# Attention probabilities turned by VectorE in 32x32 blocks and placed by a trip through DRAM, in place of TensorE transposes and copies

## The chip, the cores and the metric

The kernel runs on one core of one Trainium2 chip. The metric is the device time of the whole program in microseconds (us). Before the change it is 2019.93 us, the median of three runs from 2014.48 to 2020.14 us.

The names used below: TensorE (PE) does the matrix products, VectorE (DVE), ScalarE (ACT) and GpSimd (POOL) do the work on elements, and SyncE (SP) issues nearly all transfers, in the order of its own queue. SBUF is the memory on the chip that the engines work in, PSUM holds what TensorE writes, DRAM is the memory off the core. The granted clock is the share of TensorE's full clock that the throttle let it have.

## The reference, cut to what matters

The program is one layer of a hybrid encoder for 1024 tokens of width 1024: a layer norm, one projection to 11776 columns, dilated attention in three groups, a gated recurrence (HGRN2), a merge, a second norm and a SwiGLU feed-forward block. The change touches the attention alone. In the reference, for each group (a window and a dilation) and each of eight heads:

```python
s = jnp.einsum('nbqhd,nbkhd->nbhqk', qb, kb) * (dh ** -0.5)
s = jnp.where(valid, s + bias, NEG_INF)
mx = jnp.max(s, axis=-1, keepdims=True)
p = jnp.exp(s - mx)
l = jnp.sum(p, axis=-1, keepdims=True)
o = jnp.einsum('nbhqk,nbkhd->nbqhd', p, vb) / jnp.transpose(l, (0, 1, 3, 2, 4))
...
w = jax.nn.softmax(jnp.stack(lses), axis=0)
o = jnp.sum(w[..., None] * jnp.stack(outs), axis=0)
```

Everything is in float32.

## The kernel before

**The large products.** Every big product is split into three float32r products (hi by hi, hi by lo, lo by hi), in `mm3` (lines 275 to 279): three TensorE instructions of 128x128 weights by 512 columns for each 128 rows of depth. The projection is computed with a seven-product scheme on 2x2 blocks: `stream` (from line 677) walks over 23 groups of four column tiles, and for each group and each of two halves `g` it does seven products of 12 instructions. I call 12 such instructions a **step**; a group is 14 steps. For each half the four weight blocks a11, a12, a21 and a22 (256 KB each) are loaded on SP's queue by `block` (L256 is the load), when the block that held the place has been used. For the product numbered 6 VectorE first adds and subtracts blocks (L717, L718), so that it needs a11, a21 and a22; ScalarE then makes the hi part (L219) and GpSimd the lo part (L229). The results leave PSUM through VectorE or ScalarE into one of three `evh` buffers and are stored to DRAM on SP's queue (L578, L592, L605, L620).

**The side units.** While the projection streams, `phase1` runs side units between the steps: two recurrence units and two attention units for each of four pairs of heads. A unit is a generator; `yield 2` in it means that its next part is emitted two steps later. The order that the engines get is made from this by a list scheduler with priorities, so instructions of a unit can be put later than they were emitted.

**Attention of a pair j of heads.** `att_far` handles the two dilated groups, and `att_near` the undilated one. In each, TensorE computes scores with the queries on the partitions (L885, L902; near L1032 to L1035), VectorE adds the bias and takes the row maximum (`ttr`, L826), ScalarE takes the exponential in place with the row sums (L922; near L1051). The far probabilities lie in six tiles named `pf` (three of 1024 columns, two of which 896 columns and one of which 256 columns are used), the near ones in four tiles `p` of 1024 columns. The product with V needs the keys on the partitions, so every 128x128 block is turned first: `turn1` and `turn2` (L932, L940) for the far side and a loop at L1091 for the near side do it with 40 and 32 TensorE transposes a pair, 288 in all. They go to PSUM banks of the pool `sd` (four banks for all side units), and `copied` brings them back into the tile they came from, half of them by VectorE (L843), half by ScalarE (L841). Then come the products with V (far L963, L968, L972; near L1107) and, on the far side, a small product that reorders the row statistics (L987).

**What is queued where.** SP's queue holds the weight loads, the stores of `evh`, and the fetches for the side units, in one order; each of its transfers may wait for a semaphore, and those behind it wait as well.

Of the kernel before, what the change touches and what calls it, by code (L numbers as in the profile page):

```python
# [10 lines left out]
F32 = mybir.dt.float32  # L11
# [9 lines left out]
T = 1024  # L21
# [58 lines left out]
class Block:  # L80
    evac_ahead = 1000

    def __init__(self, ctx, tc, x, ln_in_g, ln_in_b, w_in, hgrn_lb, hgrn_norm_g, w_att_up, w_hgrn_up,
# [8 lines left out]
        nc = self.nc  # L92
# [24 lines left out]
                     for j in range(4)]  # L117
        for h in range(8):
            self.hg_d[h]["v"] = dram.tile([T, 128], F32, name=f"hg{h}v")
        for j in range(4):  # L120
            self.at_d[j].update({("v", g): dram.tile([T, 128], F32, name=f"at{j}v{g}") for g in range(3)})
        self.w_d = [dram.tile([32, 128], F32, name=f"wd{j}") for j in range(4)]
# [681 lines left out]
    def fetch_rows(self, n, name, src, g=0):  # L804
# [49 lines left out]
    def att_far(self, j, qk):  # L854
# [68 lines left out]
                                             accum_out=l[:, hd, c:c + 1])  # L923
        nc.vector.tensor_add(L12, L12, LB)
        yield 2
        yield 2

        def turn1(r):
            for hd in range(2):
                ps, p = self.ps_sd(), P1(r, hd)  # L930
                for n in range(3):
                    nc.tensor.transpose(ps[:, 128 * n:128 * n + 128], p[:, 128 * n:128 * n + 128], ident)  # L932
                self.copied(hd, p, ps[:, 0:384])

        def turn2(r0):
            for hd in range(2):
                ps = self.ps_sd().rearrange("p (r e c) -> p r e c", r=2, e=2)
                for r in range(2):
                    for e in range(2):
                        nc.tensor.transpose(ps[:, r, e], P2(r0 + r, hd)[:, e], ident)  # L940
                for r in range(2):
                    self.copied(hd, P2(r0 + r, hd), ps[:, r])
# [12 lines left out]

        kw = dict(skip_group_check=True)
        O = [self.ps_sd(), self.ps_sd()]
# [46 lines left out]
    def att_near(self, j, pre):  # L1004
# [8 lines left out]
        P = []  # L1013

        def rows(tt, hd):

# [5 lines left out]
        for b in range(4):  # L1022
            pss = [self.ps_sd().rearrange("p (t c) -> p t c", t=2) for _ in range(2)]
            P.append(self.slot((3, 4, 5, 8)[b], "p0", (2, 2, 256)))
            if b == 0:
                nc.gpsimd.memset(P[0][0:64, :, 0, 128:256], 0.0)
                nc.gpsimd.memset(P[0][64:128, :, 0, 0:128], 0.0)
            for tt in (2 * b, 2 * b + 1):
                for hd, ps in enumerate(pss):
                    pb = HD[hd]  # L1030
                    if tt == 0:
                        nc.tensor.matmul(ps[64:128, 0, 128:256], q[pb, 0:64], k[pb, 0:128], start=True, stop=True)  # L1032
                        nc.tensor.matmul(ps[0:64, 0, 0:128], q[pb, 960:1024], k[pb, 896:1024], start=True, stop=True)
                    else:
                        nc.tensor.matmul(ps[:, tt % 2, :], q[pb, 128 * tt - 64:128 * tt + 64],  # L1035
                                         k[pb, 128 * (tt - 1):128 * (tt + 1)], start=True, stop=True)
            for hd, ps in enumerate(pss):
                bi = bias[hd]
                for tt in (2 * b, 2 * b + 1):
                    o = P[b][:, hd, tt % 2, :]  # L1040
                    if tt == 0:
                        self.ttr(o[64:128, 128:256], ps[64:128, 0, 128:256], bi[64:128, 128:256], M0[64:128, hd, 0:1])
                        self.ttr(o[0:64, 0:128], ps[0:64, 0, 0:128], bi[0:64, 0:128], M0[0:64, hd, 0:1])
                    else:
                        self.ttr(o, ps[:, tt % 2, :], bi[:, 0:256], M0[:, hd, tt:tt + 1])
            s = slice(2 * b, 2 * b + 2)
            nc.vector.tensor_scalar(N0[:, :, s], M0[:, :, s], -QSCALE, None, op0=OP.mult)
            for hd in range(2):
                for tt in (2 * b, 2 * b + 1):
                    for p, z in rows(tt, hd):  # L1050
                        nc.scalar.activation(z, z, AF.Exp, bias=N0[p, hd, tt:tt + 1], scale=QSCALE,  # L1051
                                             accum_out=L0[p, hd, tt:tt + 1])
# [29 lines left out]
        def tile(tt, hd):  # L1082
            return P[tt // 2][:, hd, tt % 2, :]

        for b in range(4):
            for hd in range(2):
# [974 lines left out]
```

## Time and profile before

| What | Value |
|---|---|
| Median of 3 runs | 2019.93 us (2014.48 to 2020.14) |
| The profiled execution's own time | 2021.5 us, its span 2019.7 us |
| TensorE busy | 1985.0 us, 98% of the span |
| VectorE, ScalarE, GpSimd busy | 66%, 46%, 50% |
| Granted clock, mean | 0.997 |
| Transfers | 301.16 MB in 369404 packets |

The profiled execution is 1.6 us above the median. "Busy" is the time in which an engine has an instruction running; TensorE's instructions overlap, so the time that one of them adds is read from the distance between starts, not from its duration. The groups in the profile go by line of the kernel's source. The attention of the four pairs lies near 260 to 350 us, 505 to 590, 748 to 835 and 985 to 1085 us.

### The profile page before, as it was taken

What the parts mean: (1) busy time and instruction counts of PE and PEld (TensorE: products, weight loads), DVE (VectorE), ACT (ScalarE), POOL (GpSimd) and SP (SyncE); (2) the same over time, 40 slices, a digit from 0 to 9 for tenths busy, and PEclk for the clock granted to TensorE, in tenths of its full rate; (3) what the DMA queues carried; (4) which work ended last, traced back from release to release, by engine and by line L of the source; (5) the groups of instructions that cost most, each with busy time, mean ns of one, the idle gap of its engine ahead of it and who ended that gap; (6) DMA issues with size and microseconds to landing.
All of it is one profiled execution on the core that took longest, in us unless ns stands there. A gap on an engine that the chain in (4) does not pass through costs nothing. (4 is left out here: it accounts for less than half of the span.)

```text
span 2019.7 us, 30761 instructions
## 1 busy us (share of the span) xinstructions
PE 1985.0 (98%) x10782; PEld 1644.0 (81%) x10782; DVE 1338.9 (66%) x2105; ACT 932.7 (46%) x1926; POOL 1008.1 (50%) x874
## 2 busy tenths in 40 slices
PE   7999999999999999999999999999999999999998
PEld 5688888788888888788888888887788888888886
DVE  7876645885468944778454236557776776767788
ACT  6654455554555536555464332345333333344541
POOL 5566644576446663566546562244665665620000
PEclk9999999999999999999999999999999999999999
DMA  5444545455454453445537377434434443447533
GB/s 161 138 129 140 168 113 146 127 145 170 118 149 137 135 164 104 150 136 143 152 106 210 120 254 244 149 122 145 138 131 136 138 140 129 138 166 280 167 101 124
DMA packets 369404, 301.16 MB, mean 149 GB/s; under 512 B 98721, under 2 KB 308578, under 8 KB 369250
## 3 DMA queue, kind: packets, MB, share of 16 engines
q1 hardware_dynamic: 362752, 277.94, 45.7%
q10 hardware_dynamic: 6498, 21.27, 2.8%
q8 instruction: 85, 1.39, 0.3%
q14 instruction: 69, 0.57, 0.1%
HBM read 204.96 MB, written 94.18 MB: 148 GB/s over the span
## 5 line engine op out<-in xcount | busy, mean ns | idle before, releaser
L229 POOL TENSOR_TENSOR w_lo<-wa,w_hi 128x512 fp32r<-128x512 f32 x272 | 363.4, 1345 | 268.9 <-ACT w_hi L219 255.3
L219 ACT CAST w_hi<-wa 128x512 fp32r<-128x512 f32 x272 | 168.2, 620 | 242.9 <-PE pj L278 147.3
L229 POOL TENSOR_TENSOR w_lo<-wsum,w_hi 128x512 fp32r<-128x512 f32 x88 | 127.5, 1460 | 111.9 <-PE sd L279 60.7
L229 POOL TENSOR_TENSOR w_lo<-f_raw,w_hi 128x512 fp32r<-128x512 f32 x66 | 101.1, 1540 | 51.6 <-ACT w_hi L219 50.4
L215 POOL TENSOR_TENSOR mv<-mv,mhalf 128x1 f32<-128x1 f32 x16 | 12.6, 790 | 221.7 <-DVE mv L214 221.6
L219 ACT CAST w_hi<-wsum 128x512 fp32r<-128x512 f32 x88 | 54.6, 621 | 116.7 <-PE sd L278 107.0
L277 PE MATMUL pj<-xt1hi,w_hi 128*128 128x512 f32 x252 | 100.0, 397 | 0.7 <-DVE evh L589 0.7
L219 ACT CAST gwsum<-a_raw 128x512 fp32r<-128x512 f32 (+1 forms) x78 | 48.2, 618 | 112.4 <-PE pj L278 50.1
L278 PE MATMUL pj<-xt1lo,w_hi 128*128 128x512 f32 x252 | 98.5, 391 | 0.0
L279 PE MATMUL pj<-xt1hi,w_lo 128*128 128x512 f32 x252 | 98.2, 391 | 0.0
L719 POOL TENSOR_TENSOR wa<-wa,wa 128x512 f32<-128x512 f32 x46 | 66.2, 1440 | 57.9 <-DVE wa L718 51.6
L603 DVE TENSOR_TENSOR evh<-wkeep,pj 128x512 f32<-128x512 f32 x45 | 30.8, 685 | 89.0 <-PE pj L279 52.6
L229 POOL TENSOR_TENSOR w_lo<-ws,w_hi 128x512 fp32r<-128x512 f32 x46 | 61.8, 1348 | 55.3 <-ACT w_hi L219 50.7
L747 ACT COPY wkeep<-pj 128x512 f32<-128x512 f32 x136 | 79.6, 585 | 0.2 <-DVE evh L577 0.2
L277 PE MATMUL pj<-xt2hi,w_hi 128*128 128x512 f32 x192 | 76.6, 400 | 2.0 <-ACT w_hi L219 2.0
L279 PE MATMUL pj<-xt2hi,w_lo 128*128 128x512 f32 x192 | 76.3, 397 | 2.2 <-POOL w_lo L229 2.2
L229 DVE TENSOR_TENSOR gwkeep<-a_raw,gwsum 128x512 fp32r<-128x512 f32 (+1 forms) x78 | 53.2, 682 | 37.4 <-ACT gwsum L219 34.7
L277 PE MATMUL pj<-xb11hi,w_hi 128*128 128x512 f32 x192 | 75.9, 398 | 1.5 <-DVE evh L619 1.5
L278 PE MATMUL pj<-xt2lo,w_hi 128*128 128x512 f32 x192 | 76.1, 396 | 0.7 <-DVE xt2lo L409 0.6
L277 PE MATMUL pj<-xt4hi,w_hi 128*128 128x512 f32 x192 | 75.9, 395 | 0.0
L279 PE MATMUL pj<-xb11hi,w_lo 128*128 128x512 f32 x192 | 75.4, 393 | 0.0
L278 PE MATMUL pj<-xb11lo,w_hi 128*128 128x512 f32 x192 | 75.4, 393 | 0.0
(441 smaller groups left out, 6506.0 us busy)
## 6 DMA issues: line engine op xcount, KB each, us to landing
wa<-in_w_in_dram SPq DMA_DIRECT2D x184, 256.0 KB, 3.4
f_raw<-in_w_ffn_in_dram SPq DMA_DIRECT2D x44, 512.0 KB, 4.2
a_raw<-gd SPq DMA_DIRECT2D x30, 512.0 KB, 3.7
gd<-fc SPq DMA_DIRECT2D x44, 256.0 KB, 2.0
gd<-fs SPq DMA_DIRECT2D x33, 256.0 KB, 2.1
tg<-evh SPq DMA_DIRECT2D x32, 256.0 KB, 3.3
tg<-tg SPq DMA_DIRECT2D x16, 512.0 KB, 5.6
y<-ahs SPq DMA_DIRECT2D x16, 512.0 KB, 7.8
```

Of the source, the lines that this page charges most:

```text
L215: nc.gpsimd.tensor_tensor(mv[:, 2:3], mv[:, 2:3], self.mhalf[:, 0:1], OP.pow)
L219: ins = nc.scalar.copy(hi, src) if eng_hi == "act" else nc.vector.tensor_copy(hi, src)
L229: ins = e.tensor_sub(lo, src, hi.bitcast(F32))
L277: nc.tensor.matmul(ps, whi, xhi, start=first, stop=False, **kw)
L278: nc.tensor.matmul(ps, whi, xlo, start=False, stop=False, **kw)
L279: self.product = nc.tensor.matmul(ps, wlo, xhi, start=False, stop=last, **kw).ins.name
L603: self.left(nc.vector.tensor_add(t, add, ps))
L719: nc.gpsimd.tensor_sub(a["a21"], a["a22"], a["a11"])
L747: nc.scalar.copy(t, ps)
```

## The change

The transposes and their copies go. In their place:

- `flipped(t, scr)`: VectorE turns all 32x32 blocks of a tile in place with one instruction, and one transfer writes the tile to a scratch tensor in DRAM (`pd`, ten for each pair, as large as the tiles).
- `back(moves)`: four transfers per tile, one for each group of 32 partitions, read the scratch back into the same tile so that block (a, b) of every 128x128 block lands at (b, a). Each moves pieces of 32 numbers (128 bytes) that are contiguous on both sides.

On the far side all six tiles are flipped two steps after the exponentials were emitted, read back two steps later, and the products with V are emitted three steps after that. On the near side a tile is flipped behind its own exponentials, two tiles at a time are read back two steps later, and the products follow after the row statistics with `yield 2` and `yield 3`. All of these transfers are issued on SP's queue.

```diff
+        self.pd = [[dram.tile([128, n], F32, name=f"pd{j}{i}") for i, n in enumerate((T,) * 7 + (896, 896, 256))] for j in range(4)]
...
+    def flipped(self, t, scr):
+
+        self.nc.vector.transpose(t, t)
+        self.nc.sync.dma_start(scr, t)
+        z = scr.rearrange("(a i) (k b j) -> b i k a j", a=4, b=4, j=32)
+        return [(t[32 * b:32 * b + 32, :].rearrange("i (k a j) -> i k a j", a=4, j=32), z[b]) for b in range(4)]
+
+    def back(self, moves):
+        for dst, src in moves:
+            self.nc.sync.dma_start(dst, src)
...
         yield 2
+        moves = [self.flipped(tiles[n][:, :self.pd[j][4 + i].shape[1]], self.pd[j][4 + i]) for i, n in enumerate((2, 3, 4, 5, 8, 9))]
         yield 2
-
-        def turn1(r):
-            for hd in range(2):
-                ps, p = self.ps_sd(), P1(r, hd)
-                for n in range(3):
-                    nc.tensor.transpose(ps[:, 128 * n:128 * n + 128], p[:, 128 * n:128 * n + 128], ident)
-                self.copied(hd, p, ps[:, 0:384])
...
-        turn1(0)
-        turn1(1)
-        yield 1
-        turn1(2)
-        turn2(0)
-        yield 1
-        turn1(3)
-        turn2(2)
+        for z in moves:
+            self.back(z)
         perm = self.half("perm")
         nc.sync.dma_start(perm, self.tabs[:, 128:640])
-        yield 2
+        yield 3
...
+            moves.append(self.flipped(P[b].rearrange("p h t c -> p (h t c)"), self.pd[j][b]))
             if b % 2:
                 yield 2
+                for z in moves[b - 1:]:
+                    self.back(z)
...
-        for b in range(4):
-            for hd in range(2):
-                ps = self.ps_sd()
-                for tt in (2 * b, 2 * b + 1):
-                    for e in (0, 128):
-                        o = 256 * (tt % 2) + e
-                        nc.tensor.transpose(ps[:, o:o + 128], tile(tt, hd)[:, e:e + 128], ident)
-                self.copied(hd, P[b][:, hd].rearrange("p t c -> p (t c)"), ps)
-            if b % 2:
-                yield b
+        yield 3
```

The order of the instructions moves with it, on TensorE and on SP. The place is the far side of the fourth pair. TensorE first; `pj` are the banks of the large products, `sd` those of the side units, `tabs_sb` is the identity matrix, `NL` the row statistics. Before, the last transposes are followed at once by the products with V, all in one block:

```order
L278 MATMUL pj<-xb11lo,w_hi 128x512
L940 MATMUL sd<-tabs_sb,pf 128x128 x8
L963 MATMUL sd<-pf,v_10268 64x128 x4
L968 MATMUL sd<-pf,v_10271 64x64 x8
L972 MATMUL sd<-pf,v_10268 64x128 x4
```

Now there are no transposes, and the products with V are cut into pieces between the large products of the next group:

```order
L953 MATMUL sd<-pf,v_10119 64x128 x2
L977 MATMUL sd<-NL,perm 128x32 x4
L280 MATMUL pj<-xt2hi,w_lo 128x512
L953 MATMUL sd<-pf,v_10119 64x128 x2
L958 MATMUL sd<-pf,v_10122 64x64 x8
L962 MATMUL sd<-pf,v_10119 64x128 x4
L278 MATMUL pj<-xt2hi,w_hi 128x512
L279 MATMUL pj<-xt2lo,w_hi 128x512
L280 MATMUL pj<-xt2hi,w_lo 128x512
```

Counted in steps from the last far score, the last piece stood after 8.9 steps and stands after 13.0 now (in the four pairs: 8.7, 8.8, 8.8, 8.9 before and 14.0, 13.2, 13.0, 13.0 now). On the near side, from the first score to the last piece, it is 10.0, 10.0, 10.0, 9.9 steps before and 10.6, 9.0, 9.8, 9.5 now.

SP's queue at the same place: `tg` are stores of results of the projection, `wa` the weight blocks. Before, the loads of weight blocks stand between stores of the group that is being computed:

```order
L256 DMA wa_10252<-in_w_in_dram 128x4x128
L256 DMA wa_10361<-in_w_in_dram 128x4x128
L256 DMA wa_10381<-in_w_in_dram 128x4x128
L605 DMA tg_84<-evh 128x512
L256 DMA wa_10403<-in_w_in_dram 128x4x128
L605 DMA tg_86<-evh 128x512
L256 DMA wa_10425<-in_w_in_dram 128x4x128
L605 DMA tg_83<-evh 128x512
```

Now the second a22 block of that group (`wa_10335`; before it was `wa_10425`) stands behind the last of the 24 reads, and those behind stores (`tg_87`, `tg_89`) of the group that will use it:

```order
L832 DMA pf<-pd_216 32x28x32
L832 DMA pf<-pd_217 32x28x32
L606 DMA tg_87<-evh 128x512
L832 DMA pf<-pd_217 32x28x32 x3
L832 DMA pf<-pd_218 32x8x32
L606 DMA tg_89<-evh 128x512
L832 DMA pf<-pd_218 32x8x32 x3
L257 DMA wa_10335<-in_w_in_dram 128x4x128
L257 DMA wa_10540<-in_w_in_dram 128x4x128
```

So that block's load moved past about six stores and all the new transfers; it stood nine steps ahead of the product that needs it, and stands one step ahead now. The same holds in the third pair; in the first pair both a12 blocks and both a22 blocks (and one a21) come behind the reads, two to five steps ahead of their use.

More of the change, by code (lines that the diff above doesn't have):

```diff
@@ L925, in att_far @@
         yield 2
+        moves = [self.flipped(tiles[n][:, :self.pd[j][4 + i].shape[1]], self.pd[j][4 + i]) for i, n in enumerate((2, 3, 4, 5, 8, 9))]
         yield 2
-        def turn1(r):
-            for hd in range(2):
-                ps, p = self.ps_sd(), P1(r, hd)
-                for n in range(3):
-                    nc.tensor.transpose(ps[:, 128 * n:128 * n + 128], p[:, 128 * n:128 * n + 128], ident)
-                self.copied(hd, p, ps[:, 0:384])
-        def turn2(r0):
-            for hd in range(2):
[L937 to L942, printed above, removed]
-        turn1(0)
-        turn1(1)
-        yield 1
-        turn1(2)
-        turn2(0)
-        yield 1
-        turn1(3)
-        turn2(2)
+        for z in moves:
+            self.back(z)
         perm = self.half("perm")
         nc.sync.dma_start(perm, self.tabs[:, 128:640])
-        yield 2
+        yield 3
         kw = dict(skip_group_check=True)
@@ L1012, in att_near @@
         yield 1
-        P = []
+        P, moves = [], []
         def rows(tt, hd):
@@ L1083, in tile @@
             return P[tt // 2][:, hd, tt % 2, :]
-        for b in range(4):
-            for hd in range(2):
-                ps = self.ps_sd()
-                for tt in (2 * b, 2 * b + 1):
-                    for e in (0, 128):
-                        o = 256 * (tt % 2) + e
-                        nc.tensor.transpose(ps[:, o:o + 128], tile(tt, hd)[:, e:e + 128], ident)
-                self.copied(hd, P[b][:, hd].rearrange("p t c -> p (t c)"), ps)
-            if b % 2:
-                yield b
+        yield 3
         O = [self.ps_sd(), self.ps_sd()]
```

## The prediction

> **What bounds the kernel now.** I read the busy times first, then the clock, then what TensorE waits for, then the two stretches of the fourth pair.
>
> ```profile
> span 2019.7 us, 30761 instructions
> PE 1985.0 (98%) x10782; PEld 1644.0 (81%) x10782; DVE 1338.9 (66%) x2105; ACT 932.7 (46%) x1926; POOL 1008.1 (50%) x874
> PEclk9999999999999999999999999999999999999999
> ```
>
> TensorE is busy for 98% of the span at full clock. In the projection it hardly waits; its six reasons to wait sum to under 10 us, of which these are the longest:
>
> ```profile
> PE pj L279 <- POOL w_lo L229: 3.4, 3, 2.0
> PE pj L277 <- DVE evh L589: 1.9, 2, 1.2
> PE pj L277 <- DVE evh L619: 1.5, 1, 1.5
> ```
>
> So whatever leaves TensorE's queue shortens the program by the time that it added there, and whatever makes TensorE wait lengthens it. The stretches that the change touches, first the far and then the near side of the fourth pair (columns: window, us, busy us of PE, PEld, DVE, ACT and POOL, then clock, share of the DMA engines, GB/s):
>
> ```profile
> 985.00:1030.00 45.00, 45.00 (x361) 37.19 (x361) 20.11 (x70) 26.64 (x77) 18.31 (x14) 1.00 0.39 112
> 1030.00:1085.00 55.00, 54.80 (x353) 44.87 (x352) 31.56 (x80) 29.56 (x74) 22.88 (x19) 1.00 0.52 149
> ```
>
> TensorE is full in both; VectorE has 25 and 23 us free; the DMA engines are at 0.39 and 0.52. The change moves work from the engine that has no room to two that have some.
>
> **What is removed.** Starts tell what twelve and eight transposes add between large products:
>
> ```profile
> 279.17 1.47 PE L932 MATMUL sd<-tabs_sb,pf 128*128 128x128 f32 x12
> 280.40 0.48 PE L277 MATMUL pj<-xt1hi,w_hi 128*128 128x512 f32 x1
> ...
> 1024.60 1.03 PE L940 MATMUL sd<-tabs_sb,pf 128*128 128x128 f32 x8
> 1025.56 0.66 PE L963 MATMUL sd<-pf,v 128*64 128x128 f32 x8
> 1026.99 0.66 PE L963 MATMUL sd<-pf,v 128*64 128x128 f32 x8
> ```
>
> Twelve add 1.23 us (279.17 to 280.40), 0.103 each; eight add 0.96, 0.12 each. I take 0.106: 288 x 0.106 = **31 us** off TensorE. This is the whole gain. The 48 copies go too, which frees VectorE and ScalarE, on neither of which TensorE waits much.
>
> **What VectorE gets.** Ten turns for each pair, 5120 columns far and 4096 near. Its rate is in this row, beside the copies it loses:
>
> ```profile
> L589 DVE STREAM_TRANSPOSE evh<-evh x30: 648/700/715, 80.1 to 958.8; 128x512 f32<-128x512 f32 x30
> L843 DVE COPY pf<-sd x32: 385/484/558, 279.8 to 1025.6; 128x384 f32<-128x384 f32 x16, 128x256 f32<-128x256 f32 x16
> L843 DVE COPY p<-sd x16: 648/682/695, 332.8 to 1065.8; 128x512 f32<-128x512 f32 x16
> ```
>
> At 0.70 us for 512 columns, 1.4 us for a full tile, the turns are 7.0 us far and 5.6 near; the copies that leave are 8 x 0.484 = 3.9 and 4 x 0.682 = 2.7. VectorE gains 3 us in each stretch, with 23 to 25 free: I cost it at nothing. Behind a turn stand evictions of `evh`, for which TensorE waits; the cover is the 2.72 us of a step below, in which an eviction may be 1.4 us late once. If the cover failed every time it would be 40 x 1.4 = 56 us; the rows of 1.9 and 1.5 us in the whole projection say it seldom does.
>
> The Trainium skill ("VectorE: DVE Perf Modes", "Rules for kernel authors") prefers TensorE for a 128x128 transpose that may land in PSUM. By that rule the removed path was the cheaper one; but the rule prices the one transpose, and in this case's rows TensorE is at 98% and VectorE at 66%, so that the engine that does it matters more than the cost.
>
> **What the queue and the DMA engines get.** For each pair ten writes (2.62 MB far, 2.10 near) and forty reads in pieces of 128 bytes (20480 packets far, 16384 near), all on SP's queue. POOL's queue carries none of them. No row of the profile is a read of 128-byte pieces only. The nearest are a window with stores in small packets alone (423.4 to 425.6 us, 64 KB each), one dense window (404.6 to 405.8), one with weight loads in 512-byte packets (436 to 440) and one with large packets (434 to 436, the second queue):
>
> ```profile
> DMA packets 1630, 0.20 MB, mean 92 GB/s; under 512 B 1630, under 2 KB 1630, under 8 KB 1630
> q1 hardware_dynamic: 1630, 0.20, 62.4%
> ...
> q1 hardware_dynamic: 1637, 0.26, 122.2%
> ...
> q1 hardware_dynamic: 1944, 0.96, 84.6%
> ...
> q10 hardware_dynamic: 138, 0.50, 65.6%
> ```
>
> A small packet takes 16 engines x 2.2 us x 0.624 / 1630 = **13.5 ns** of one engine; in the dense window 16 x 1.2 / 1637 = 11.7 ns (the packets overlap there, hence the 122%). A 512-byte one takes 16 x 4 x 0.846 / 1944 = **27.9 ns**, so a weight block of 256 KB takes 0.92 us of all sixteen. Large packets take 16 x 2 x 0.656 / 16 / 0.50 = 2.6 us for a MB, so a store of `evh` (256 KB) takes 0.69.
>
> Far: 20480 x 13.5 / 16 = 17.3, writes 2.62 x 2.6 = 6.9, in all **24.2 us** for one pair (21.9 at 11.7 ns; 35.7 + 6.9 = 42.6 at 27.9). Near: 13.8 + 5.5 = **19.3** (17.5; 34.1). The Trainium skill ("DMA: Bandwidth & Descriptors", "Specifications") asks for 512 bytes in a transfer for the full rate and says that smaller ones are read, changed and written. The trace agrees that they are slow, 128 bytes in 13.5 ns against 512 in 27.9, half the rate. By 512-byte cost for each packet the time would be the rival's that is priced from the 27.9 ns row below.
>
> **Is it in time?** A step is 12 large products:
>
> ```profile
> 1815.22 0.91 PE pj L277 x4
> 1817.94 0.91 PE pj L277 x4
> ```
>
> 2.72 us. *Far, pair four.*
>
> ```profile
> L902 PE MATMUL sd<-k,q x64: 269/269/320, 994.6 to 996.4; 64*64 64x128 f32 x64
> L922 ACT ACTIVATE pf<-pf,NL x22: 386/450/563, 999.8 to 1014.0; 128x320 f32<-128x320 f32 x10, 128x192 f32<-128x192 f32 x6, 128x128 f32<-128x128 f32 x6
> ...
> at1v<-evh SPq DMA_DIRECT2D x3, 64.0 KB, 2.0
> ```
>
> The exponentials start 3.4 us after the last score and run 14.5 us. In the code's order the first whole tiles stand after 14 of the 22, at 9.2 us; with a turn, transfers start at 10.6. In that stretch pass also about seven stores (7 x 0.69 = 4.8) and a weight block (0.9), so the engines are through at 10.6 + 24.2 + 5.7 = 40.5, landed some 2.0 later (the last row): 42.5 us after the first exponential. TensorE reaches the last piece 13 steps after the last score: 13 x 2.72 - 3.4 = 32.0, plus 3.8 for the pieces ahead of it (two of 1.43 us, 1025.56 to 1026.99, and 0.9 of reordering) = 35.8. The wait is 6.7 us; 4.4 with the dense packets; 0 if those also hide the stores. I take 5, nearest to the dense row since these reads come dense, in three pairs, and 2.5 in the first, which has one step more: **17.5 us**.
>
> *Near, pair four.*
>
> ```profile
> L1035 PE MATMUL sd<-k,q x28: 376/376/480, 1038.7 to 1047.2; 64*128 64x256 f32 x28
> L1051 ACT ACTIVATE p<-p,N x18: 397/502/515, 1044.7 to 1055.0; 128x256 f32<-128x256 f32 x14, 64x128 f32<-64x128 f32 x4
> ```
>
> A quarter of the exponentials is done 2.7 us after 1044.7, so the first tile is turned 10 us after the first score. Then 19.3 + three stores (2.1) + four weight blocks (3.7) = 25.1, landed at 37. TensorE is at the last piece after 9.5 steps (25.8) and 2 us of products: 27.8. The wait is 9.2; it is 7.4 with dense packets, 1.6 if the stores and weights do not count, and 0 if the pieces come in step with the reads. I take the middle of 0 and 9, rounded down, 4 in each of four: **16 us**.
>
> **Clock.** A wait of TensorE costs more than itself here:
>
> ```profile
> 853.06 0.39 PE L278 MATMUL pj<-xb22lo,w_hi 128*128 128x512 f32 x1
> 855.47 0.50 PE L279 MATMUL pj<-xb22hi,w_lo 128*128 128x512 f32 x1 [2.03 <-POOL w_lo L229]
> 856.63 0.63 PE L277 MATMUL pj<-xb22hi,w_hi 128*128 128x512 f32 x1
> 857.06 0.63 PE L278 MATMUL pj<-xb22lo,w_hi 128*128 128x512 f32 x1
> ...
> 856.00:858.00 2.00, 2.00 (x7) 1.53 (x7) 2.00 (x3) 0.00 (x0) 2.00 (x4) 0.59 0.45 131
> 858.00:860.00 2.00, 2.00 (x7) 1.58 (x6) 2.00 (x4) 0.62 (x1) 2.00 (x4) 0.56 0.33 95
> ```
>
> After 2.03 us of waiting the granted clock is 0.59 and 0.56, and starts are 0.43 apart instead of 0.227. Some 3.4 us at that clock lose 1.7. Of eight waits some will be cut into pieces between which products run; I count three such drops, **5 us** (none to eight: 0 to 14). The Trainium skill ("TensorE: Matmul & The Clock Gate", "HAM oscillation — how this bites in real kernels") puts the bound at gaps over about 3.4 us; here 2.03 already did it, and the row decides. By the page's bound the far waits still count and the near ones would not.
>
> **Weight blocks** now stand behind the reads on SP's queue, the second a22 of the third and fourth pair one step (2.72 us) ahead of its product. A landing takes 2.8 us at least, 3.4 at the median, and hi and lo parts follow, so these can be late. But the same reads hold up the products with V, which come first: a late block here mostly stands beside a wait already counted. I cost it at nothing, and put the other case among the rivals.
>
> ```profile
> DMA to landing us min/median/max: 2.8/3.4/6.6
> ```
>
> **Sum.** Against the profiled execution, whose own time is 2021.5 us (1.6 above the median): 2021.5 - 31 + 17.5 + 16 + 5 = 2029; less 1.6, **2027 us**.
>
> **Rivals.** *A, the transfers are hidden* (the other side: faster). The wait at the product vanishes once the transfers end 6.7 us sooner far and 9.2 near. For it: the DMA engines are at 0.39 and 0.52, the dense row saves 2.3 and 1.8, and stores and weight blocks that fall outside the stretch save 5.7 and 5.8, together 8.0 and 7.6. Against: the reads of a tile wait for its own write to land. Far nothing is left, near 1.6 x 4 = 6: 2021.5 - 31 + 6 - 1.6 = **1995 us** (1989 with nothing left). *B, a read of 128 bytes costs what 512 do*, 27.9 ns: far 18.4 us more, near 14.8, 33 for each pair, 133 in all, on a path that waits already: 2027 + 133 = **2160**, or about 2120 where the queue's stores overlap. For it: at 512 bytes the packet already costs only twice that of 128, so that bytes are not what sets it. Against: the 1630 packets at 13.5. *C, SP's queue in order*: the late a22, a12 and a21 blocks of three pairs are waited for by themselves, 2.8 + 0.6 + 1.4 us (landing, hi part, lo part) less 2.7, about 2.1 at each of some seven blocks with a drop of the clock each: 7 x (2.1 + 1.7) = 27, **2054**. The change not doing what it says is out: the transposes are gone from TensorE's order.
>
> ```profile
> L219 ACT CAST w_hi<-wa 128x512 fp32r<-128x512 f32 x272 | 168.2, 620 | 242.9 <-PE pj L278 147.3
> L229 POOL TENSOR_TENSOR w_lo<-wa,w_hi 128x512 fp32r<-128x512 f32 x272 | 363.4, 1345 | 268.9 <-ACT w_hi L219 255.3
> ```
>
> **How the numbers follow.** Forecast 0.50, A 0.27, B 0.15, C 0.08. The forecast's own range is 2006 (waits of 17 us, no drop) to 2060 (all waits at their upper ends, 6.7 x 3 + 4.2 + 9.2 x 4 = 61, and 10 of drops). The range over all is 1990 to 2085: it leaves out B and a part of A. About 0.3%, 6 us, is what a measurement of this kernel can tell. Within the forecast's range lie 0.08 below 2014, 0.15 up to 2026 and 0.27 above. Faster: 0.27 + 0.08 = 0.35; same 0.15; slower 0.27 + 0.15 + 0.08 = 0.50.
>
> **What would show it.** The saving: TensorE's busy time falls by about 37 us, the distance of large products across the old places by 31. The waits: idle of TensorE ahead of the products of `pf` and `p` with `v`, 2 to 7 us each, released by a transfer, and a clock under 1 behind them. A: no such idle, and a span near 1993. B: the reads take over 20 ns a packet in their window. C: idle ahead of large products, released by the hi or lo part of a weight block. I am wrong if the reads run much faster than 11.7 ns, or if TensorE finds other work in its order before it comes to a product that waits.

## The result, and the profile after

The changed kernel takes 2089.49 us, the median of four runs (2084.36 to 2095.67); the kernel before, beside it, 2018.59 (2014.48 to 2020.14). The ratio is 1.0356, 95% interval 1.0316 to 1.0395: **71 us slower**. I had predicted 2027 us with a range from 1990 to 2085, and slower with a chance of 0.50. The sign was forecast at even odds only; the size was not. Single executions on record that took 2545 us and more (one of the kernel in experiment 6, one of that in 11, one of the kernel before beside 9 to 12) lie far outside all others and are left out of every time below.

The changed kernel's busy times over the whole span, and the wait reasons of TensorE in the projection (65 us from the start to its end); columns of a wait row: us in total, times, longest.

```profile
span 2082.6 us, 30435 instructions
PE 1987.1 (95%) x10494; PEld 1629.7 (78%) x10494; DVE 1364.3 (66%) x2097; ACT 914.9 (44%) x1878; POOL 1008.8 (48%) x874
```

```profile
PE sd L953 <- DMA pf<-pd: 17.7, 7, 3.8
PE sd L1091 <- DMA p<-pd: 11.6, 8, 3.6
PE pj L278 <- DVE evh L604: 6.6, 1, 6.6
PE pj L278 <- DVE evh L589: 5.9, 1, 5.9
PE pj L278 <- DVE evh L620: 4.4, 2, 3.5
PE pj L278 <- ACT wkeep L748: 4.3, 1, 4.3
PE pj L278 <- ACT w_hi L220: 3.7, 4, 2.0
PE sd L1022 <- DMA q<-at1q: 3.2, 1, 3.2
...
PE sd L1091 <- issue: 1.4, 1, 1.4
```

The two first rows and the last are waits at the products with V, 30.7 us; for the last, of 1.4 us, the profile names no releaser, and I count it to the reads because it stands among products that wait for them. But more than half of the waiting stands elsewhere: ahead of large products that need a free bank or a weight block's hi part, and ahead of side products that need a fetched tile. All reasons together sum to 71.3 us, against 9.3 before.

The whole projection, first before (to 1153.4 us), then after (to the same product, at 1216.7), us, busy us of PE, PEld, DVE, ACT and POOL, clock, share of the DMA engines, GB/s:

```profile
65.00:1153.40 1088.40, 1078.98 (x6759) 898.80 (x6758) 688.51 (x1237) 561.72 (x1298) 621.11 (x565) 1.00 0.49 141
```

```profile
65.00:1216.70 1151.70, 1080.44 (x6460) 883.93 (x6459) 713.36 (x1225) 541.01 (x1245) 620.36 (x565) 0.98 0.63 166
```

The difference of the two stretches, 1151.7 - 1088.4 = 63.3 us, is the whole difference of the spans (62.9; the profiled execution of the changed kernel is its fastest of four, so that the medians lie 71 apart). TensorE's idle grew by 61.8 us (71.3 less 9.4). Its busy time is 1.5 us longer although 288 transposes are gone, which added 29.4 us between starts (12.7 near, 9.3 and 7.3 far, summed over the trace of before). So 30.9 us came back as slower work: the granted clock stood at half in ten stretches of the projection, 54.6 us in all, against one of 3.4 us before. If all of the 51.2 us more had been work, half of it, some 25 us, would be the loss; the rest, some 5, is then left for products that now stand in small pieces between large ones (experiment 1 has 3.5 for it).

One place shows waiting and clock together. It is after the near side of the second pair, first TensorE, then VectorE ahead of it, then the clock:

```profile
636.48 0.39 PE L280 MATMUL pj<-xb11hi,w_lo 128*128 128x512 f32 x1
642.75 0.77 PE L278 MATMUL pj<-xb11hi,w_hi 128*128 128x512 f32 x1 [5.88 <-DVE evh L589]
643.31 0.63 PE L279 MATMUL pj<-xb11lo,w_hi 128*128 128x512 f32 x1
643.74 0.63 PE L280 MATMUL pj<-xb11hi,w_lo 128*128 128x512 f32 x1
```

```profile
620.46 0.75 DVE L1097 TENSOR_TENSOR near<-near,sd 128x448 f32<-128x448 f32 x2 [15.72 <-DMA near<-wd]
...
634.74 2.31 DVE L1165 TENSOR_TENSOR_SCAN fa<-fa,d 128x512 f32<-128x512 f32 x1
636.98 0.66 DVE L1188 SCALAR_TENSOR_TENSOR qd<-q,fa 128x512 f32<-128x512 f32 x1
637.57 3.35 DVE L1183 RECIPROCAL qd<-fa 128x256 f32<-128x256 f32 x2
640.84 1.19 DVE L1165 TENSOR_TENSOR_SCAN fb<-fb,d 128x528 f32<-128x528 f32 x1
641.95 0.65 DVE L589 TENSOR_TENSOR evh<-wkeep,pj 128x512 f32<-128x512 f32 x1
```

```profile
640.00:650.00 10.00, 7.25 (x26) 5.96 (x27) 10.00 (x11) 1.67 (x4) 4.28 (x5) 0.66 0.25 76
```

TensorE waits 5.88 us for an eviction that stands on VectorE behind the scans and reciprocals of the recurrence. VectorE had stood idle for 15.72 us, until the broadcast of `near` for the merge landed; from there to the eviction it has one more gap, of 1.41 us for `rl`, and in its order the scans stand behind the merge. That broadcast and the recurrence's inputs `t` were issued behind the reads of `p` (issue rows of SP's queue: start, us, times; first before, then after):

```profile
579.02 1.11 SPq L1077 DMA_DIRECT2D near<-wd  x2
...
592.56 2.36 SPq L801 DMA_DIRECT2D t<-hg4t  x2
```

```profile
608.72 5.38 SPq L832 DMA_DIRECT2D p<-pd  x7
614.20 1.51 SPq L1070 DMA_DIRECT2D near<-wd  x2
...
617.09 0.53 SPq L802 DMA_DIRECT2D t<-hg4t  x1
...
625.90 0.33 SPq L802 DMA_DIRECT2D t<-hg4t  x1
```

The large products of that place ran 14 to 19 us later than before (by the starts of the same products up to the wait), the broadcast 35 us later, the fetches 25 and some 31, so TensorE had moved 5 us and more ahead of all three. In the first and third pair it is the merge of the near side as well (L1097, L1100, which use the broadcasts of `near` and `rl`, issued behind the reads) that stands ahead of the eviction, and the wait is 4.3 and 3.5 us; in the fourth it is 6.6 us, and the room for the next stage's `evh` comes late, when the last attention result has been stored (VectorE waits 8.79 us for `near` and 8.18 for that store). At the far side of the second pair SP's queue looks like this:

```profile
548.07 2.19 SPq L621 DMA_DIRECT2D hg4g<-evh  x1
550.31 13.59 SPq L832 DMA_DIRECT2D pf<-pd  x17
564.01 4.50 SPq L257 DMA_DIRECT2D wa<-in_w_in_dram  x6
```

For 13.59 us SP issues nothing but 17 reads, 0.80 us each; then six weight loads go out in one row. In that stretch the DMA engines are full (share 1.22, as packets overlap):

```profile
550.30:563.90 13.60, 11.80 (x78) 9.04 (x78) 3.18 (x9) 2.35 (x4) 3.28 (x4) 1.00 1.22 141
```

VectorE waited 4.2 us in all for weight blocks ahead of L717 before, and 37.9 after (L718). What a read holds on the queue is in the rows of its line (issue: ns least, median, most):

```profile
L832 SPq DMA_DIRECT2D pf<-pd x96: 557/687/2710, 282.4 to 1086.9; - x96
L832 SPq DMA_DIRECT2D p<-pd x64: 557/725/2273, 340.1 to 1132.7; - x64
```

All issues of the trip, reads and writes, hold SP for 154 us in the projection; everything else that SP issues there takes 323, and took 286 before.

### The profile page after: what moved, and what is told of

Same layout as the page of the kernel before. It is cut to its first block, busy times and chain, and to the rows that moved or that the text cites. A ratio compares the mean times of both kernels' runs of the same rounds, so it can differ in the third digit from the quotient of the medians.

```text
span 2082.6 us, 30435 instructions
## 1 busy us (share of the span) xinstructions
PE 1987.1 (95%) x10494; PEld 1629.7 (78%) x10494; DVE 1364.3 (66%) x2097; ACT 914.9 (44%) x1878; POOL 1008.8 (48%) x874
## 5 line engine op out<-in xcount | busy, mean ns | idle before, releaser
L216 POOL TENSOR_TENSOR mv<-mv,mhalf 128x1 f32<-128x1 f32 x16 | 12.7, 792 | 221.7 <-DVE mv L215 221.6
L748 ACT COPY wkeep<-pj 128x512 f32<-128x512 f32 x136 | 79.2, 582 | 32.1 <-PE pj L280 29.4
L718 DVE TENSOR_TENSOR ws<-wa,wa 128x512 f32<-128x512 f32 x46 | 45.6, 991 | 55.7 <-DMA wa<-in_w_in_dram 37.9
```

The lines of the kernel that those rows point to most:

```text
L216: nc.gpsimd.tensor_tensor(mv[:, 2:3], mv[:, 2:3], self.mhalf[:, 0:1], OP.pow)
L718: self.behind(nc.vector.tensor_add(a["s1"], a["a21"], a["a22"]))
L748: nc.scalar.copy(t, ps)
```

## The experiments

All times are medians; beside each stands the kernel before, run on the same chip (2017.0 to 2021.4 us). The ratio is to that, with its 95% interval. Differences between experiments are of times; by the ratios they can be some 3 us larger or smaller.

**1. What the removal is worth without the trip.** `back` does nothing, `flipped` only turns.

```diff
-        self.nc.sync.dma_start(scr, t)
...
-        for dst, src in moves:
-            self.nc.sync.dma_start(dst, src)
+        return
```

> The turns by VectorE stay, the write to DRAM and the reads back are left out, so the products with V read blocks that are turned but not placed (the output is not the reference's). TensorE's order has the same products and no transfer to wait for. It tells what the removal of 288 transposes is worth without the trip. All theories of the loss put it into the trip: 2018.6 - 31 = about 1988 us, with no more than 10 us of half clock in the projection. If it stays over 2010, the saving of 31 us itself was wrong (the products with V in small pieces, or VectorE's turns ahead of evictions, take it back).

2003.5 us, ratio 0.9915 (0.9901 to 0.9930): 18 us are gained, not 31. The projection's row:

```profile
65.00:1135.40 1070.40, 1053.09 (x6470) 868.53 (x6469) 707.24 (x1229) 541.39 (x1250) 627.48 (x565) 1.00 0.50 143
```

TensorE's idle is 17.3 us here (9.4 before) and its busy time falls by 25.9, not by 29.4: the new order of the same work gives 8 us back as waits and some 3.5 in products that are cut into pieces. So the trip costs 2089.5 - 2003.5 = 86 us (89 by the ratios).

**2. Reads that nothing waits for.** `pd2` is a second scratch in DRAM.

```diff
-        return [(t[32 * b:32 * b + 32, :].rearrange("i (k a j) -> i k a j", a=4, j=32), z[b]) for b in range(4)]
+        w = self.pd2[tuple(scr.shape)]
+        return [(w[32 * b:32 * b + 32, :].rearrange("i (k a j) -> i k a j", a=4, j=32), z[b]) for b in range(4)]
```

> All writes and all 160 reads of 128-byte pieces stay on SP's queue, but the reads land in a second scratch in DRAM, so no product waits for them (the blocks are left unplaced, the output is not the reference's). Theory P (the loss is the wait at the products with V, 30.7 us in the trace of the changed kernel, and the half clock behind it): about 1990 us, as without the trip. Theory Q (the reads fill SP's queue, 17 of them in one row of 13.59 us, and weight blocks, stores of evh and the fetches of the recurrence behind them come late; TensorE then waits 4.3 to 6.6 us at one place in each pair): the waits of 4 to 7 us ahead of large products stay, 2035 to 2060 us.

2062.0 us, 1.0205 (1.0188 to 1.0222). 58 of the 86 us stay though no product waits for a read. The waits are all elsewhere:

```profile
PE pj L279 <- DVE evh L605: 11.3, 1, 11.3
PE pj L281 <- POOL w_lo L231: 5.5, 5, 1.7
PE sd L1024 <- DMA k<-at1k: 4.5, 1, 4.5
```

This ends theory P, which was my prediction's: the wait at the products is the smaller part. A reservation: these reads also write DRAM, so they are not quite the same transfer.

**3. The reads on ScalarE's queue.**

```diff
-            self.nc.sync.dma_start(dst, src)
+            self.nc.scalar.dma_start(dst, src)
```

> The 160 reads are issued on ScalarE's queue in place of SP's; nothing else changes. Packets and bytes are the same. Theory Q (SP's queue in order): weight blocks, stores and fetches come in time again, the waits of 4 to 7 us ahead of large products go, 2030 to 2055 us, unless ScalarE's own evictions are held up behind reads that wait for their write. Theory R (the packets fill the 16 DMA engines, whoever issues them): every transfer is late as before, 2080 to 2095 us. Theory P: the waits at the products stay, 2080 to 2095.

2086.8 us, 1.0327 (1.0311 to 1.0342), as the change. SP was rid of the reads, but ScalarE now issues them between its own work and waits with them:

```profile
805.75 9.71 ACTq L832 DMA_DIRECT2D pf<-pd  x8
815.52 0.63 ACT L605 ACTIVATE evh<-evh 128x512 f32<-128x512 f32 x1 [12.69 <-DMA pf<-pd]
816.29 0.62 ACT L220 CAST w_hi<-wa 128x512 fp32r<-128x512 f32 x1
```

TensorE waits 6.02 us for the hi part made behind them. The longest wait, 16.5 us, comes at the end of the fourth pair, where VectorE waits 14.42 us for the broadcast of `near` and 8.13 for the last store. The cost was moved to another queue; this run alone cannot tell queue from packets.

**4. Whole rows in place of pieces**, same bytes, same 160 reads.

```diff
-        return [(t[32 * b:32 * b + 32, :].rearrange("i (k a j) -> i k a j", a=4, j=32), z[b]) for b in range(4)]
+        return [(t[32 * b:32 * b + 32, :], scr[32 * b:32 * b + 32, :]) for b in range(4)]
```

> The same writes and the same 160 reads of the same bytes in the same places of SP's queue, but each read moves whole rows of 4096, 3584 or 1024 bytes, so that the blocks come back unplaced (the output is not the reference's). It has a small part of the packets. Theory R (packets): the reads take half the time or less, and most of the loss goes, below 2030 us. If the loss lies in the trip itself (a write, a landing, a read, a landing) or in the number of transfers on the queue: 2060 to 2090 us. Theory Q in its present form (17 reads in 13.59 us, 0.80 us each, which is 1024 packets at about 12.5 ns on 16 engines) expects the first.

2039.8 us, 1.0087 (1.0072 to 1.0102): 50 of the 86 us go with the small pieces. It was less than theory R expected. The pieces change two things at once, the packets and the issue, which takes 0.42 us in place of 0.69:

```profile
L832 SPq DMA_DIRECT2D pf<-pd x96: 302/420/1096, 285.2 to 1046.0; - x96
```

**5 and 6. One side alone** (`att_near` or `att_far` as before the change).

> The far side as changed, the near side as before (transposes and copies). Measured so far: the change 71 us over the kernel before, of which the removal without the trip gives 18 back, so the trip costs about 86. If the cost goes by packets (20480 far, 16384 near) the far trip costs 48 and its removal gives about 10: 2018.6 + 38 = about 2057 us. If the near side carries most of it (its end gives the rooms to the recurrence, whose work stands ahead of evictions on VectorE): under 2040 us.

> The near side as changed, the far side as before. By packets the near trip costs 38 and its removal gives about 8: about 2048 us. If the near side carries most of it: over 2065 us. If the two sides hinder each other (reads of one behind the other): both runs together add less than 71 us to the kernel before.

Far alone 2052.8 us, 1.0163 (1.0138 to 1.0189); near alone 2041.6, 1.0112 (1.0090 to 1.0134). They add 34 and 23 us, 57 together, 14 less than the change with both, so the two sides hinder each other a little; their ratio is near to that of their reads (96 and 64). Neither side pays for itself.

**7. The writes alone.**

```diff
-        for dst, src in moves:
-            self.nc.sync.dma_start(dst, src)
+        return
```

> The turns and the 40 writes to DRAM stay, all reads are left out (the products read unplaced blocks, the output is not the reference's). The writes are 18.9 MB in large packets, about 49 us of all 16 DMA engines in the whole program. If reads are the cost: 2003.5 + 0 to 8 us. If it is the bytes, or the write's wait for its turn at the head of SP's queue: 2015 us or more.

2004.8 us, 0.9930 (0.9909 to 0.9951): the writes cost 1 us (3 by the ratios, whose intervals overlap). Nearly the whole cost is in the reads.

**8. A quarter of the packets**, all 160 reads.

```diff
-        ... (t[32 * b:32 * b + 32, :].rearrange("i (k a j) -> i k a j", a=4, j=32), z[b]) ...
+        ... (t[32 * b:32 * b + 8, :].rearrange("i (k a j) -> i k a j", a=4, j=32), z[b][0:8]) ...
```

> All writes and all 160 reads in their places on SP's queue, waited for by the products as in the change, but each read moves 8 of its 32 partitions: a quarter of the 128-byte packets (most blocks stay unplaced, the output is not the reference's). Theory Q' (the entries on SP's queue and the trip's latency, not the packets): 2070 us or more, near the change. Theory R (the packets fill the DMA engines and every transfer beside them is late): the cost over the 2003.5 us without the trip falls to a quarter of 86 or a little more, 2025 to 2040 us. With the wide pieces at 2040 us it separates the packets from the bytes: below 2040 means that the bytes of the wide pieces cost too.

2070.7 us, 1.0251 (1.0232 to 1.0270). Three quarters of the small packets are gone and only 19 us with them, so theory R is not the main thing. The rows of the reads and one stretch of SP's queue:

```profile
L832 SPq DMA_DIRECT2D pf<-pd x96: 655/657/1869, 287.3 to 1072.8; - x96
...
300.55 6.27 SPq L832 DMA_DIRECT2D pf<-pd  x9
```

Nine reads in a row take 0.70 us each, while the DMA engines stand at 0.39 of their time in that stretch. So the issue has a price of its own, which the number of pieces, from 256 to 1024, does not set: a read with 256 pieces holds the queue for 0.66 us even at the least, one with 1024 for 0.56 at the least and about 0.7 at the median. By these least values the quarter reads are themselves the dearer ones to issue, by 0.1 us each, 16 in all; this run gives less back than the packets alone cost.

**9. Twice the issues**, the same packets.

```diff
         for dst, src in moves:
-            self.nc.sync.dma_start(dst, src)
+            for h in (slice(0, 16), slice(16, 32)):
+                self.nc.sync.dma_start(dst[h], src[h])
```

> Each read is cut into two of 16 partitions: 320 reads in place of 160, the same packets, bytes and places. Theory I (what costs is the issue: a read of small pieces holds its queue 0.69 us, 0.66 even with a quarter of the packets, against 0.42 with whole rows, and what stands behind it on the queue comes late): 160 more issues of 0.66 us, 40 and 26 us... that is 16 us far and 11 near for each pair, put the loss from 86 us to 150 or more: 2140 to 2200 us. Theory R (packets): no change, 2080 to 2100 us.

2184.1 us, 1.0821 (1.0797 to 1.0845): 95 us more for 160 issues more, 0.59 us for each. The bytes and, within a few thousand, the packets are those of the change. This is what theory I asked for. Waits of TensorE sum to 134 us, and half clock to 181 us.

**10. Half of the reads on each queue.**

```diff
-        for dst, src in moves:
-            self.nc.sync.dma_start(dst, src)
+        for n, (dst, src) in enumerate(moves):
+            (self.nc.scalar if n % 2 else self.nc.sync).dma_start(dst, src)
```

> Every second read is issued on ScalarE's queue, the others stay on SP's: the issue time on each queue is halved, the packets are the same. Theory I: the reads pass both queues in half the time (some 8 us far and 6 near in place of 17 and 11), the products wait for little, 2025 to 2060 us, less what ScalarE's evictions lose behind reads that wait for their write. Theory R: as the change, 2080 to 2095 us. With all reads on ScalarE's queue 2086.8 us were measured, where theory I says that ScalarE's evictions and hi parts stood behind them instead.

2077.9 us, 1.0299 (1.0275 to 1.0323): only 11 us better, a miss. SP's queue in the second pair:

```profile
544.66 12.99 SPq L832 DMA_DIRECT2D pf<-pd  x10
...
DMA packets 14169, 2.15 MB, mean 165 GB/s; under 512 B 13916, under 2 KB 14030, under 8 KB 14169
```

Ten reads take 12.99 us, 1.30 each, while ScalarE issues five: 0.87 us for a read over both queues, no less than the 0.80 of one. The second row is the same stretch: 16 x 12.99 us / 13916 = 14.9 ns for a small packet on each engine, and the engines are full (1.22). Here the packets hold both queues.

**11. No turns either** (as 1, and `vector.transpose` left out).

> Neither trip nor turns (the probabilities stay as they were, the output is not the reference's): the transposes and copies are out and nothing comes in. With the turns it was 2003.5 us. If VectorE's turns cost nothing, as was predicted, it stays within 3 us of that; if they hold up evictions, it falls to about 1990, which is the kernel before less the 29.4 us that the transposes add between starts in its trace.

1998.1 us, 0.9905 (0.9881 to 0.9928), against 0.9915 (0.9901 to 0.9930) with the turns. The two are not told apart: VectorE's turns cost at most a few us (5 by the times, 2 by the ratios).

**12. Reads in portions**, with two more steps to the products.

```diff
-        for z in moves:
-            self.back(z)
+        for i, z in enumerate(moves):
+            self.back(z)
+            if i in (1, 3):
+                yield 1
...
-                for z in moves[b - 1:]:
-                    self.back(z)
+                self.back(moves[b - 1])
+                yield 1
+                self.back(moves[b])
```

> The reads are emitted in portions: on the far side two tiles, a step, two tiles, a step, two tiles; on the near side one tile of each two, a step, the other. The products come two and two steps later in each pair. Theory I: weight blocks and fetches get between the portions and the products have two steps (5.4 us) more, so waits of 2 to 4 us at the products and at weight blocks go: 2035 to 2065 us. If only the sum of the queue's time counts: 2080 us or more.

2082.4 us, 1.0317 (1.0295 to 1.0338). The far products' wait falls to 4.5 us, but others take its place (near 18.6, the recurrence's L1244 12.8). So it seems to be the sum of the queue's time that counts, more than its spacing.

**13. A quarter of the packets and two queues** (8 and 10 together).

> Both edits at once: a quarter of the packets (8 of the 32 partitions of each read, most blocks unplaced, the output is not the reference's) and every second read on ScalarE's queue. Alone they brought 2070.7 and 2077.9 us, beside the change's 2089.5. Theory D (two limits that lie close together hold up the reads: the issue, 0.66 us for each on one queue, and the packets, 1024 x 11.7 to 13.5 ns / 16 = 0.75 to 0.86 us for each on the engines; lifting one leaves the other): together they bring far more than the sum of 19 and 11, down to 2020 to 2045 us, as the wide pieces did (2039.8). Theory I alone (SP's queue): 2089.5 - 19 - 11, about 2060 us or more.

2051.9 us, 1.0163 (1.0134 to 1.0192). That is 38 us below the change, where 19 and 11 add to 30: a little more than the sum, but not the 2020 to 2045 of theory D. In the rows, though, the mechanism that D names is there:

```profile
L832 SPq DMA_DIRECT2D pf<-pd x48: 655/662/1271, 286.6 to 1058.2; - x48
L832 ACTq DMA_DIRECT2D pf<-pd x48: 665/667/885, 286.6 to 1052.8; - x48
```

With few packets both queues issue at their 0.66 us side by side. A read on SP that overlaps one on ScalarE takes 0.67 us at the median, one that does not 0.66. So the two queues do not share the issue; what slowed them in experiment 10 is the packets. The Trainium skill ("DMA: Bandwidth & Descriptors", "Issuing engines are not separate DMA queues") says the same: transfers of all queues end up on the same 16 engines, and a second queue only saves the time of the issue, which it calls usually small beside the transfer. The runs agree with the first part (14.9 ns for a packet with two queues, 14.4 with one); the second does not hold for these transfers, where the issue (0.56 to 0.66 us) comes near to the packets (896 to 1024 at 14.4 ns on 16 engines, 0.81 to 0.92 us). The largest wait left in this run is at the near products (18.0 of 49.6 us).

**14. One read of whole rows for each tile**, 40 reads.

```diff
-        return [(t[32 * b:32 * b + 32, :].rearrange("i (k a j) -> i k a j", a=4, j=32), z[b]) for b in range(4)]
+        return [(t, scr)]
```

> One read of whole rows of 128 partitions for each tile, 40 reads in place of 160, few packets, all bytes (the blocks come back unplaced, the output is not the reference's). With 160 reads of whole rows it was 2039.8 us at 0.42 us for each issue. Theory D: 120 issues less of 0.42 us, 50 us of SP's queue, leave the trip's own latency: 2008 to 2025 us. If the latency of the trip (turn, write, landing, read, landing) is what the 2039.8 consist of: 2030 us or more.

2036.5 us, 1.0080 (1.0055 to 1.0106), 3 us below the 160 reads of whole rows, within their intervals. So 120 issues fewer hardly matter any more at 0.42 us (92 us of issue for the trip there, 43 here); a reservation is that the larger reads land later (5.2 to 6.7 us after their issue, against 3.8 to 4.0). 33 us over the kernel without the trip remain, with neither many issues nor small pieces. TensorE's waits sum to 37.7 us here (10.9 of them at the near products), against 16.9 without the trip.

**15. The near side alone, products three steps later.**

```diff
-        yield 3
+        yield 6
         O = [self.ps_sd(), self.ps_sd()]
```

> The near side alone as changed (2042.6 us), with its products emitted three steps later (8.2 us). If the loss of the near side were the wait of TensorE at its products, it falls to about 2015 us, below the kernel before; if it is the reads' hold on SP's queue and the later end of the unit, it stays at 2030 to 2045 us.

2030.0 us, 1.0053 (1.0038 to 1.0067): 11.5 us better than near alone, still slower than before. No wait at the products is left; these are:

```profile
PE pj L278 <- DVE evh L590: 6.9, 2, 6.2
PE pj L280 <- POOL w_lo L230: 5.7, 6, 1.6
PE pj L278 <- ACT w_hi L220: 5.6, 1, 5.6
PE pj L278 <- DVE evh L620: 3.3, 2, 2.9
```

The distance can hide the trip from the products, not from the rest of the queue. No version that was run, with all blocks in their places, beats the kernel before.

## Why the prediction was right or wrong

Beside each term what was measured:

| Term of the sum | Predicted | Measured |
|---|---|---|
| Transposes off TensorE | -31 | -29.4 between starts; -18 net, with the new order (experiment 1) |
| Turns on VectorE | 0 | a few us at most (1 against 11) |
| Writes | in the transfers | 1 to 3 (7) |
| Waits at the far products | 17.5 (2.5, 5, 5, 5) | 17.7 (2.9, 1.8, 8.3, 4.7) |
| Waits at the near products | 16 (4 each) | 13.0 (3.6, 2.5, 3.1, 3.7) |
| Waits elsewhere | 0 (15 in rival C) | 31 more than before (71.3 - 30.7 - 9.3), of which 8 come without the trip too (experiment 1) |
| Clock | 5 | about 25 (51.2 us more at half) |

**The waits at the products were right in place and in sum**, 30.7 us against 33.5. That the far sum fits to 0.2 us is luck: the second pair waited 1.8 us and the third 8.3, where 5 was given to each. In the fourth pair the far wait was 2.74 and 1.96 us against 5:

```profile
1082.93 0.76 PE L953 MATMUL sd<-pf,v 128*64 128x128 f32 x5 [2.74 <-DMA pf<-pd]
...
1086.82 0.66 PE L953 MATMUL sd<-pf,v 128*64 128x128 f32 x8 [1.96 <-DMA pf<-pd]
...
1093.03 0.50 PE L278 MATMUL pj<-xt2hi,w_hi 128*128 128x512 f32 x1 [1.98 <-ACT w_hi L220]
```

**The packet's price was nearly right**, so rival B was not the case. In a stretch of reads alone (552 to 560 us):

```profile
DMA packets 8896, 1.12 MB, mean 140 GB/s; under 512 B 8896, under 2 KB 8896, under 8 KB 8896
```

16 x 8 / 8896 = 14.4 ns for a packet on each engine, against the 11.7 to 13.5 that I used and the 27.9 of rival B.

**The step that failed first is the account of SP's queue: what stands behind the reads was put at nothing.** I counted a read as a load on the engines, which delays the products with V, and not as an entry that holds SP; of what comes behind I weighed the weight blocks alone, and wrote "I cost it at nothing". The reads hold SP for 0.7 us each at the median, 131 us in all; 160 more issues with the same packets cost 95 us (experiment 9), and when no product waits for a read, 58 of the 86 us stay (2). Behind the reads stand the weight blocks, the stores that free `evh`, the fetches of the next unit and the broadcasts for the merge, and the waits at other places, put at nothing, are 31 us (8 of them come without the trip too). The late block beside 1093.03 above is a wait of its own, not one that stands beside a wait already counted. Rival C named this place and a price of 2.1 us each, but saw only the weight blocks. It left out the fetches of the recurrence and the broadcasts, behind which come 3.5 to 6.6 us in one wait in each pair: their work on VectorE comes late and has evictions behind it. I had looked at what is late next in the queue and not at what the late unit does on another engine.

**The clock was mis-sized.** Half clock does follow waits, but the number of drops was wrong: ten stretches of 3.4 to 10.2 us, not three of 3.4. I had counted the waits that I had priced; the others brought theirs. "After 2.03 us" is no threshold either: in the trace of the change every wait of 2.88 us or more has a drop at it, while single ones of 1.80, 1.83, 1.98 and 2.38 us (at 559.74, 481.73, 1093.03 and 617.98) have none. The bound of the Trainium skill that I set beside it in the prediction ("TensorE: Matmul & The Clock Gate", "HAM oscillation — how this bites in real kernels"), gaps over about 3.4 us, did not hold in this trace: a wait of 2.88 us (at 312.46), and waits of 2.74 and 1.96 us that lie close together, brought a drop. By that bound the near waits of 4 us would have counted as well; the prediction said that they would not.

**The saving was mis-sized by the order.** 29.4 us between starts is near to 31, but only 18 of them arrive when the trip is taken away, because the same products in another order wait 8 us more, and TensorE's busy time falls by 3.5 us less than the 29.4. I had costed the new order at nothing.

**Rival A** was wrong: the transfers are hidden from no side. What spoke for it, the DMA engines at 0.39 and 0.52, was a mean over a stretch of the kernel before; while the reads go out it is 1.22 (550.3 to 563.9 us), and SP's queue is held for 13 us at a time.

**What the time follows.** It moves with the sum for which the reads hold SP's queue, added up over the rows of their line: 130.9 us in the change, 208.7 with twice the issues (experiment 9), 111.7 with a quarter of the packets (8), 71.8 with whole rows (4). 78 us more cost 95, 19 less gave 19 back, 59 less gave 50. With 40 reads (14) it is 22.9, 49 less again, and that gave only 3.

**What the runs do not settle.** Two parts of the 86 us are shown: the small pieces (some 50, experiment 4, by issue and packets together) and the remaining 33 to 36 with whole rows. How much of the small pieces' part is issue and how much packets was not measured apart. An estimate from the least hold of a read, 0.56 us: 160 x 0.56 = 89 of the 131 us would be the issue alone and 42 the packets that push back. That the remaining 33 are the latency of the trip (turn, write, landing, read, landing) and the later end of the units is argued from the waits in experiment 14, not shown by a run that takes only that away.

## What to carry to other kernels

Price a transfer three times: by its packets on the engines, by its landing, and by the time that its issue holds the queue, with a list of everything that stands behind it in that queue; where the queue also feeds the bounding engine, the third can be the largest. When TensorE has no room to spare, count each wait of some 3 us, and shorter ones that lie close together, with the half clock that follows, and each unit that ends later with what its late work does to evictions on the other engines. To find the part that matters, first leave the new path out entirely and measure the gross gain: here it was 18 us, against a path with 154 us of issues on the queue that also loads the weights.

## What the runs showed of the hardware

The issue of a read in 128-byte pieces takes 0.66 us on SP and 0.67 on ScalarE with 256 pieces, and no less than 0.56 with 1024; a read of whole rows with the same bytes takes 0.30 at the least and 0.42 at the median. A 128-byte packet takes 14.4 ns of each engine in a dense row of reads from one queue and 14.9 from two (experiment 10). Two queues issue side by side at full rate as long as the packets leave room (experiment 13); when they do not, two are no faster than one (0.87 us for a read against 0.80). Half clock came in stretches of 3.4 us and multiples of it (3.4, 6.8 and 10.2 us in the changed kernel).
